# Row 0 of the first x transfer as a transfer of its own, ahead of rows 1 to 3, with y left whole

## Chip, cores, metric

One core of a Trainium2 chip. The metric is the device time of one execution in microseconds (us), the lower the better. All runs told of here were in the undisturbed ("fast") state. A difference of under 2% counts as "same".

## The reference

```python
x, y: float32 [1024, 4096]
out[r] = sum over c of abs(x[r, c] - y[r, c])      # float32 [1024]
```

Two inputs of 16.8 MB each go in, 4 KB come out. Almost nothing is computed per byte.

## The kernel before

Each of the 128 partitions holds 8 rows. The kernel has buffers on chip for all 8 rows of x (`xa` rows 0 to 3, `xb` rows 4 to 7), but only for 4 rows of y (`yb`). Rows 4 to 7 of y are loaded into the slots of rows 0 to 3 when those have been subtracted. VectorE subtracts in place, ScalarE takes the absolute value and sums.

```python
PIECES = [1728, 1056, 640, 384, 288]          # the last row comes in pieces
...
# first instructions of SyncE and ScalarE: 4 rows each, 64 KB a partition
put(lambda: nc.sync.dma_start(out=xa, in_=xr[:, 0:H, :]).then_inc(s_first, 16), before="RegisterMove")
put(lambda: nc.scalar.dma_start(out=yb, in_=yr[:, 0:H, :]).then_inc(s_first, 16), before="RegisterMove")
# next on SyncE: rows 4 to 6 of x, 48 KB a partition, no wait
put(lambda: nc.sync.dma_start(out=xb[:, 0:H - 1, :], in_=xr[:, H:K - 1, :]).then_inc(s_xb, 16))
for k in range(H - 1):                        # y rows 4 to 6, each when its slot is free
    put(lambda: nc.sync.wait_ge(s_sub, k + 1))
    put(lambda: nc.sync.dma_start(out=yb[:, k, :], in_=yr[:, H + k, :]).then_inc(s_row[k], 16))
...                                           # then row 7 of both in pieces
for k in range(H):
    sub(xa[:, k, :], yb[:, k, :], [(s_first, 32)] if k == 0 else [])
    absum(xa[:, k, :], ro[:, k:k + 1], s_act)
...                                           # rows 4 to 7 the same way, then 4 KB out
```

A transfer that has landed has raised its semaphore (a counter that engines wait for) by 16, so a wait for 32 on `s_first` is a wait for two whole transfers.

A transfer is cut over 16 DMA engines, 8 partitions each. What an engine moves for one partition in one transfer is one packet in the trace: 64 KB for `xa` and `yb`, 48 KB for the next x transfer.

Of the kernel before, what the change touches and what calls it, by code (L numbers as in the profile page):

```python
# [5 lines left out]

F32 = mybir.dt.float32
ABS = mybir.ActivationFunctionType.Abs
AX = mybir.AxisListType.X

F32 = mybir.dt.float32
ABS = mybir.ActivationFunctionType.Abs
AX = mybir.AxisListType.X

PIECES = [1728, 1056, 640, 384, 288]
HALVES = [2048, 2048]


class Entry:


    def __init__(self, nc):
        self.nc = nc

    def put(self, emit, before="UnconditionalBranch"):
        nc = self.nc
        hook = nc.inst_callbacks[-1]
        lower = nc._always_lower_symbolic_ap
        nc.remove_inst_callback(hook)
        nc._always_lower_symbolic_ap = False  # L30
        here = nc.cur_bb.bb.instructions
        n = len(here)
        try:
            emit()
        finally:
            nc._always_lower_symbolic_ap = lower
            nc.push_inst_callback(hook)
        here = nc.cur_bb.bb.instructions
        main = nc.main_func.blocks[0].instructions
        while len(here) > n:  # L40
            mine = here.pop(n)
            first = next(i for i, x in enumerate(main) if x.engine == mine.engine and x.opcode == before)
            main.insert(first, mine)

    def at_end(self, emit):

        nc = self.nc
        hook = nc.inst_callbacks[-1]
        here = nc.cur_bb.bb.name
        done = []  # L50

        def closing(ins):
            if done or nc.cur_bb.bb.name == here or ins.engine != mybir.EngineType.SP:
                return
            done.append(ins)
            emit()

        nc.remove_inst_callback(hook)
        nc.push_inst_callback(closing)
        nc.push_inst_callback(hook)  # L60


@with_exitstack
def kernel(ctx, tc, x, y, axis, out):
    nc = tc.nc
    P = nc.NUM_PARTITIONS
    R, C = x.shape
    K = R // P
    xr = x.rearrange("(p k) c -> p k c", p=P, k=K)
    yr = y.rearrange("(p k) c -> p k c", p=P, k=K)  # L70
    orr = out.rearrange("(p k) -> p k", p=P, k=K)
    assert sum(PIECES) == C and sum(HALVES) == C
    n_part = len(PIECES) - 1
    n2 = len(HALVES)
    H = K // 2
    entry = Entry(nc)
    put = entry.put

    def sbuf(name, shape):
        return nc.alloc_sbuf_tensor(name, shape, F32).ap()  # L80

    xa = sbuf("xa_rows", [P, H, C])
    xb = sbuf("xb_rows", [P, H, C])

    yb = sbuf("yb_rows", [P, H, C])
    ro = sbuf("ro_sums", [P, K])
    half = sbuf("half_sums", [P, 2, n2])

    last = sbuf("last_piece", [P, n_part + PIECES[-1]])

    s_first = tc.alloc_semaphore("s_first")
    s_xb = tc.alloc_semaphore("s_xb")
    s_row = [tc.alloc_semaphore(f"s_row{k}") for k in range(H - 1)]
    s_piece = [tc.alloc_semaphore(f"s_piece{i}") for i in range(len(PIECES))]
    s_sub = tc.alloc_semaphore("s_sub")
    s_act = tc.alloc_semaphore("s_act")
    s_end = tc.alloc_semaphore("s_end")
    s_out = tc.alloc_semaphore("s_out")


    put(lambda: nc.sync.dma_start(out=xa, in_=xr[:, 0:H, :]).then_inc(s_first, 16), before="RegisterMove")
    put(lambda: nc.scalar.dma_start(out=yb, in_=yr[:, 0:H, :]).then_inc(s_first, 16), before="RegisterMove")
    put(lambda: nc.sync.dma_start(out=xb[:, 0:H - 1, :], in_=xr[:, H:K - 1, :]).then_inc(s_xb, 16))
    for k in range(H - 1):
        put(lambda: nc.sync.wait_ge(s_sub, k + 1))
        put(lambda: nc.sync.dma_start(out=yb[:, k, :], in_=yr[:, H + k, :]).then_inc(s_row[k], 16))
    o = 0
    for i, w in enumerate(PIECES):
        c = slice(o, o + w)
        put(lambda: nc.sync.dma_start(out=xb[:, H - 1, c], in_=xr[:, K - 1, c]).then_inc(s_piece[i], 16))  # L110
        if i == 0:
            put(lambda: nc.sync.wait_ge(s_sub, H))
        put(lambda: nc.sync.dma_start(out=yb[:, H - 1, c], in_=yr[:, K - 1, c]).then_inc(s_piece[i], 16))
        o += w


    count = [0, 0]

    def sub(tx, ty, waits):
        for s, v in waits:  # L120
            put(lambda: nc.vector.wait_ge(s, v))
        put(lambda: nc.vector.tensor_sub(out=tx, in0=tx, in1=ty).then_inc(s_sub, 1))  # L122
        count[0] += 1

    def absum(tx, to, sem):
        put(lambda: nc.scalar.wait_ge(s_sub, count[0]))
        put(lambda: nc.scalar.activation(tx, tx, ABS, accum_out=to).then_inc(sem, 1))  # L127
        count[1] += sem is s_act

    for k in range(H):  # L130
        sub(xa[:, k, :], yb[:, k, :], [(s_first, 32)] if k == 0 else [])
        absum(xa[:, k, :], ro[:, k:k + 1], s_act)
    sub(xb[:, 0, :], yb[:, 0, :], [(s_xb, 16), (s_row[0], 16)])
    absum(xb[:, 0, :], ro[:, H:H + 1], s_act)

    for k in (1, 2):
        o = 0
        for i, w in enumerate(HALVES):
            c = slice(o, o + w)
            sub(xb[:, k, c], yb[:, k, c], [(s_row[k], 16)] if i == 0 else [])  # L140
            absum(xb[:, k, c], half[:, k - 1, i:i + 1], s_act)
            o += w
    done56 = count[1]
    o = 0
    for i, w in enumerate(PIECES):
        c = slice(o, o + w)
        tx, ty = xb[:, H - 1, c], yb[:, H - 1, c]
        if i == 2:
            put(lambda: nc.vector.wait_ge(s_act, done56))
            put(lambda: nc.vector.reduce_sum(out=ro[:, K - 3:K - 1], in_=half, axis=AX).then_inc(s_end, 1))  # L150
        if i < n_part:
            sub(tx, ty, [(s_piece[i], 32)])
            absum(tx, last[:, i:i + 1], s_end)
        else:
            put(lambda: nc.vector.wait_ge(s_piece[i], 32))
            put(lambda: nc.vector.tensor_sub(out=last[:, n_part:n_part + w], in0=tx, in1=ty).then_inc(s_end, 1))  # L156
            put(lambda: nc.vector.wait_ge(s_end, n_part + 2))
            put(lambda: nc.vector.reduce_sum(out=ro[:, K - 1:K], in_=last, axis=AX, apply_absolute_value=True).then_inc(s_end, 1))  # L158
        o += w

    put(lambda: nc.sync.wait_ge(s_end, n_part + 3))
    put(lambda: nc.sync.dma_start(out=orr, in_=ro).then_inc(s_out, 16))
    entry.at_end(lambda: nc.sync.wait_ge(s_out, 16))


# [1 line left out]
_INS = ['x', 'y', 'axis']  # L167
_OUTS = [((1024,), 'float32')]

_NUMBERS = {'axis': -1}  # L170


# [26 lines left out]
```

## Time and profile before

| | before |
|---|---|
| time, median of 3 | 85.63 us (85.59 to 85.64) |
| bytes read | 33.55 MB |
| rate over the span of 83.7 us | 401 GB/s |
| VectorE busy, ScalarE busy | 36.3 us, 31.6 us |
| first subtraction starts | 41.39 us |

The table says "limited by reading": each compute engine is idle for more than half of the span. How the single views carry that is told in the prediction. A stretch counts a packet's bytes at the packet's start, so a short stretch with long packets can show 519 or 371 GB/s for the same flow; only long stretches, or the packet records one by one, can be compared. The chain of waits names what released an instruction, not what it queued behind.

### The profile page before, as it was taken

Reading aid. Unit: us, or ns where it says so; the run is one execution under the profiler, and the core shown is the slowest. Engines: PE = TensorE matmul, PEld = TensorE weight load, DVE = VectorE, ACT = ScalarE, POOL = GpSimd, SP = SyncE. Lnnn points to the kernel's source line nnn. Section 1 sums busy time; section 2 is a strip of 40 time slices with the busy share of each in tenths; the row PEclk is TensorE's granted clock in tenths of the full one; section 3 lists DMA queues with packets and bytes.
Section 4 is the critical chain, followed back from the end, with each engine's and each line's share of the span. In section 5 each row is a group of like instructions: output and inputs, shape, how many; then the busy total and the mean of one; then the engine's idle time right before and its main releaser. Section 6 shows DMA issues by size and latency. Waiting matters only on the chain.

```text
span 83.7 us, 102 instructions
## 1 busy us (share of the span) xinstructions
DVE 36.3 (43%) x16; ACT 31.6 (38%) x27; POOL 0.2 (0%) x4
## 2 busy tenths in 40 slices
DVE  0000000000000000000299999999199898997870
ACT  5000000000000000000000979798880899999960
POOL 0000000000000000000000000000000000000000
DMA  9569999983999999669899988889999999999910
GB/s 501 219 282 501 501 501 501 501 376 157 470 501 501 501 501 438 282 282 501 376 399 634 470 376 376 376 360 438 438 399 462 407 454 377 423 409 410 392 40 2
DMA packets 2449, 33.56 MB, mean 401 GB/s; under 512 B 401, under 2 KB 913, under 8 KB 1681
## 3 DMA queue, kind: packets, MB, share of 16 engines
q1 hardware_dynamic: 2304, 25.17, 71.5%
q10 hardware_dynamic: 144, 8.39, 23.1%
q14 instruction: 1, 0.00, 0.0%
HBM read 33.55 MB, written 0.00 MB: 401 GB/s over the span
## 4 chain that ended last, share of the span: by engine, by line
DMA 68%; DVE 22%; ACT 7%; ACTq 0%; issue 0%
DMA yb_rows<-in_y_dram 68%; DVE xa_rows L122 16%; ACT xb_rows L127 7%; DVE xb_rows L122 5%; DVE ro_sums L158 1%; ACTq L194 0%
## 5 line engine op out<-in xcount | busy, mean ns | idle before, releaser
L122 DVE TENSOR_TENSOR xa_rows<-xa_rows,yb_rows 128x4096 f32<-128x4096 f32 x4 | 17.4, 4420 | 41.4 <-DMA yb_rows<-in_y_dram 41.4
L127 ACT ACTIVATE xa_rows<-xa_rows 128x4096 f32<-128x4096 f32 x4 | 14.5, 3616 | 45.5 <-DVE xa_rows L122 45.5
L122 DVE TENSOR_TENSOR xb_rows<-xb_rows,yb_rows 128x2048 f32<-128x2048 f32 (+5 forms) x9 | 17.9, 2020 | 3.4 <-DMA yb_rows<-in_y_dram 3.3
L127 ACT ACTIVATE xb_rows<-xb_rows 128x2048 f32<-128x2048 f32 (+5 forms) x9 | 15.2, 1686 | 2.9 <-DVE xb_rows L122 2.8
L127 ACT ACTIVATION_READ_ACCUMULATOR xb_rows<-xb_rows 128x1 f32 x9 | 1.7, 186 | 0.0
L127 ACT ACT_TABLE_LOAD x1 | 1.3, 1283 | 0.9 <-PEq L180 0.9
L127 ACT ACTIVATION_READ_ACCUMULATOR xa_rows<-xa_rows 128x1 f32 x4 | 0.7, 186 | 0.0
L156 DVE TENSOR_TENSOR last_piece<-xb_rows,yb_rows 128x288 f32<-128x288 f32 x1 | 0.5, 459 | 0.2 <-DMA yb_rows<-in_y_dram 0.2
L158 DVE TENSOR_REDUCE ro_sums<-last_piece 128x1 f32<-128x292 f32 x1 | 0.5, 457 | 0.1
L150 DVE TENSOR_REDUCE ro_sums<-half_sums 128x2 f32<-128x4 f32 x1 | 0.1, 150 | 0.0
L180 POOL MEMSET const-bfloat16-1.0<- 128x1 bf16 x1 | 0.1, 102 | 0.0
L180 POOL MEMSET const-uint8-127<- 128x1 uint8 x1 | 0.1, 102 | 0.0
L180 POOL MEMSET const-float32-1.0<- 128x1 f32 x1 | 0.1, 99 | 0.0
L180 POOL MEMSET const-float32-0.0<- 128x1 f32 x1 | 0.1, 98 | 0.2 <-issue 0.2
## 6 DMA issues: line engine op xcount, KB each, us to landing
xb_rows<-in_x_dram SPq DMA_DIRECT2D x1, 6144.0 KB, 54.8
yb_rows<-in_y_dram SPq DMA_DIRECT2D x3, 2048.0 KB, 15.3
xb_rows<-in_x_dram SPq DMA_DIRECT2D x1, 864.0 KB, 17.6
yb_rows<-in_y_dram SPq DMA_DIRECT2D x1, 864.0 KB, 15.8
xb_rows<-in_x_dram SPq DMA_DIRECT2D x1, 528.0 KB, 16.7
yb_rows<-in_y_dram SPq DMA_DIRECT2D x1, 528.0 KB, 17.5
xb_rows<-in_x_dram SPq DMA_DIRECT2D x1, 320.0 KB, 17.8
yb_rows<-in_y_dram SPq DMA_DIRECT2D x1, 320.0 KB, 18.1
```

The lines of the kernel that those rows point to most:

```text
L122: put(lambda: nc.vector.tensor_sub(out=tx, in0=tx, in1=ty).then_inc(s_sub, 1))
L127: put(lambda: nc.scalar.activation(tx, tx, ABS, accum_out=to).then_inc(sem, 1))
L150: put(lambda: nc.vector.reduce_sum(out=ro[:, K - 3:K - 1], in_=half, axis=AX).then_inc(s_end, 1))
L156: put(lambda: nc.vector.tensor_sub(out=last[:, n_part:n_part + w], in0=tx, in1=ty).then_inc(s_end, 1))
L158: put(lambda: nc.vector.reduce_sum(out=ro[:, K - 1:K], in_=last, axis=AX, apply_absolute_value=True).then_inc(s_end, 1))
L180: nc = _bacc.Bacc("TRN2", target_bir_lowering=False, num_devices=1)
```

## The change

The intent, as the code shows it: row 0 of x comes in short packets, so it is on chip early. The wait still asks for everything.

```diff
-    put(lambda: nc.sync.dma_start(out=xa, in_=xr[:, 0:H, :]).then_inc(s_first, 16), before="RegisterMove")
-    put(lambda: nc.scalar.dma_start(out=yb, in_=yr[:, 0:H, :]).then_inc(s_first, 16), before="RegisterMove")
+    for r in (slice(0, 1), slice(1, H)):
+        put(lambda: nc.sync.dma_start(out=xa[:, r, :], in_=xr[:, r, :]).then_inc(s_first, 16), before="Drain")
+    put(lambda: nc.scalar.dma_start(out=yb, in_=yr[:, 0:H, :]).then_inc(s_first, 16), before="Drain")
...
-        sub(xa[:, k, :], yb[:, k, :], [(s_first, 32)] if k == 0 else [])
+        sub(xa[:, k, :], yb[:, k, :], [(s_first, 48)] if k == 0 else [])
```

## The prediction

> **What bounds the kernel now.** I read the page first (busy shares, the forty slices, the DMA issues), then the chain of waits, then the transfers in stretches that I chose by where the chain breaks, and last the single packet records of the trace. The page clears the compute engines at once:
>
> ```profile
> DVE 36.3 (43%) x16; ACT 31.6 (38%) x27; POOL 0.2 (0%) x4
> ...
> DMA  9569999983999999669899988889999999999910
> ...
> HBM read 33.55 MB, written 0.00 MB: 401 GB/s over the span
> ```
>
> VectorE and ScalarE are idle more than half the time, and the DMA row is near 9 nearly everywhere. The 5, 6 and 3 in that row look like holes, but a slice is 2.09 us and a 64 KB packet takes longer than that; a whole packet is counted where it starts, so the row beats against the packet length. Stretches much longer than a packet take the beat out:
>
> ```profile
> core 0: us, DVE busy (x) ACT busy (x) POOL busy (x), PEclk, DMA share, GB/s
> 0.00:1.00 1.00, 0.00 (x0) 0.09 (x1) 0.20 (x4) 1.00 0.00 0
> 1.00:4.00 3.00, 0.00 (x0) 1.20 (x1) 0.00 (x0) 1.00 1.09 371
> 4.00:40.00 36.00, 0.00 (x0) 0.00 (x0) 0.00 (x0) 1.00 1.00 435
> 40.00:56.00 16.00, 14.61 (x4) 8.90 (x5) 0.00 (x0) 1.00 0.99 426
> 56.00:70.00 14.00, 11.72 (x4) 10.78 (x7) 0.00 (x0) 1.00 1.00 427
> 70.00:80.00 10.00, 8.84 (x8) 9.71 (x13) 0.00 (x0) 1.00 0.99 398
> ```
>
> From 1 us to 80 us the 16 DMA engines have a share of 0.99 to 1.00 (1.09 in the start is a packet counted past its stretch). There are no holes; only the rate falls, slowly, as packets get smaller towards the end. The chain of waits tells which landings matter:
>
> ```profile
> 0.13 41.24 DMA yb_rows<-in_y_dram
> 41.37 0.02 issue
> 41.39 13.11 DVE xa_rows L122 x3
> 54.49 0.02 issue
> 54.51 15.88 DMA yb_rows<-in_y_dram
> 70.39 0.02 issue
> 70.41 4.51 DVE xb_rows L122 x2
> ```
>
> It must be read with care. It says that three subtractions release a y transfer at 54.51 that lands 15.88 us later. But that transfer is 2 MB, which takes 4.9 us at 427 GB/s; the other 11 us it stands behind others in the same queue. So the subtractions are not what sets the time there; the queue is. The idle time of the first subtraction after the first rows says the same:
>
> ```profile
> L122 DVE TENSOR_TENSOR xb_rows<-xb_rows,yb_rows 128x4096 f32<-128x4096 f32 x1 | 4.4, 4424 | 1.9 <-DMA yb_rows<-in_y_dram 1.9
> ```
>
> VectorE works through the first four rows and then waits 1.9 us for the next. The first landing, taken as a signal, could slip by up to that with nothing lost. What can't slip is the stream of bytes: anything that makes it longer moves the end one for one.
>
> **What the Trainium skill says.** In "DMA: Bandwidth & Descriptors", section "Queues, rings and completion order", each DMA engine goes round between the queue rows that have work and switches only at packet boundaries. The records agree: on one engine a 64 KB packet of the SyncE queue (x) is followed by one of the ScalarE queue (y), in strict turn, each starting within 5 ns of the end of the one before. The same page, "Where 436 GB/s comes from", gives 435 GB/s for the 16 engines together; the trace has 435 in the stretch 4 to 40 us, so there is no speed left to win in steady state. Its section "Why small descriptors are slow" gives a fixed few cycles per packet; the trace shows how small that is here (below). In "Perfetto Trace Analysis", section "DMA Optimizations", splitting DMAs may help where DMA engines are idle and parts can start sooner; neither holds here, as the next part shows.
>
> **The change part by part.** Removed: one x transfer of 8 MB (128 packets of 64 KB, 8 an engine). Added: two x transfers in its place, row 0 (8 packets of 16 KB an engine) and rows 1 to 3 (8 of 48 KB an engine). Bytes, order inside the SyncE queue, and y are as before.
>
> Start position: the placement in the diff also goes from before the first RegisterMove to before the first Drain. In the built programs no RegisterMove is left and the transfers are the first instruction of SyncE and of ScalarE in both, followed by the Drain. I count 0.
>
> Compute: the instruction order of VectorE and ScalarE is unchanged. The first subtraction waits for 48 instead of 32, that is, for both x parts and y. So row 0, though it lands early, releases nothing. Gain there: 0.
>
> Issue: SyncE issues one more transfer, 0.38 us in the timeline, and reaches the barrier, and the next x transfer, that much later: at about 1.3 instead of 0.91 us. That transfer isn't served before 40 us. Cost on the path: 0.
>
> Turns: before, x and y packets alternate at equal size and finish together near 40.5 us. After, 8 turns of 16 KB against 64 KB: y is done after 8 x (607 + 2414) ns = 24.2 us of service, near 26 us, with row 0. Then the SyncE queue runs alone with rows 1 to 3 for 8 x 1812 ns = 14.5 us. A lone queue is not slower: between 40 and 56 us it is alone, with 48 KB packets at 1812 ns, that is 27.1 GB/s an engine, the same as the 64 KB packets in turn (65536 B in 2414 ns). These three paces, 2414, 1812 and 607 ns from start to start, are medians of the packet records.
>
> Sum for an engine: before 16 x 2414 = 38624 ns. After 8 x 607 + 8 x 2414 + 8 x 1812 = 4856 + 19312 + 14496 = 38664 ns, so 40 ns more, for 8 more packets. One more completion packet is 6 ns (its pace in the records). Together 0.05 us. The first subtraction should start near 41.45 instead of 41.39, and now be released by x. Every later landing moves by about the same, and so does the end: 85.63 + 0.05 = 85.68 us. I say 85.7.
>
> **The rivals.** First, the start. The first x packet of an engine takes 2.89 to 3.44 us in the records, where later ones of the same size take 2.42: some 0.65 us at the middle that steady state does not have, and the reason why the stretch 1 to 4 us moved only 371 GB/s. If that loss belongs to the first packet in proportion to its size, a 16 KB first packet loses a quarter, 0.16 us, and 0.49 us is won: 85.2 us. If it is a fixed ramp (all engines starting together, the first reads), it stays, only spread over the 16 KB packet and the y packet behind it. I hold the second likelier: no other first packet of a transfer shows an extra (the first 48 KB packet took 1815 ns like the rest), so it belongs to the moment, not to the packet. Second, unequal packets: turns by packet give y four times the bytes of x, and if an engine lost time fetching descriptors for short packets, 8 short ones an engine could cost some 0.1 us each at worst: 0.8 us, 86.5. Against it: the 16 KB packets after 55 us run alone at 607 ns with no gap. Third, an early start of compute: row 0 of x is on chip near 26 us, as is all of y, and a kernel that waited for row 0 alone could start 15 us earlier. This one doesn't, and even if it did, the queue would still set the end: the y slots would be free earlier, but the queue is never empty now. So this rival makes 85.7 as well, not less. Fourth, the placement: if something of a few tenths ran ahead of the transfers, all would move, to perhaps 86.0; the built programs speak against it.
>
> **Range and chances.** The three runs before spread over 0.05 us. The sum gives 85.7; a partly cured ramp pulls down by up to 0.5, a placement or descriptor cost pulls up by some tenths. I take 85.3 to 86.0 for 8 in 10. A 2% verdict needs 1.7 us, more than every rival above makes; within 2% gets 0.97, slower 0.02 and faster 0.01.
>
> **What would show it right or wrong.** Right: in the chain the first piece is now the x transfer, landing near 41.3 us after the issue; y lands near 26.5; the stretch 4 to 40 us still shows 435 GB/s; the wait of 1.9 us before the fifth row is still there; the last landing moves by under 0.1 us. Wrong: a faster 1 to 4 us (the ramp scales with the packet), a rate below 430 GB/s between 4 and 26 us (short packets cost) or between 26 and 40 us (x alone reads more slowly), or a first packet later than 1.0 us after the first issue (placement). A change of over 1.7 us either way would mean that the stream itself had a limit that this trace, with equal packets in two queues, did not show.

## The result, and the profile after

| | before | after |
|---|---|---|
| median of 6 runs each | 85.61 us (85.49 to 85.70) | 85.35 us (85.20 to 85.57) |
| ratio | | 0.9976, 95% interval 0.9958 to 0.9994 |
| first subtraction starts | 41.39 us | 41.09 us |

A ratio here is the mean time of one kernel's fast runs over that of the other's fast runs of the same rounds, so it isn't quite the ratio of the medians. By it the change is worth -0.2 us (85.6 x 0.0024), anywhere from -0.05 to -0.36: "same" by the 2% rule, but on the other side of zero than the predicted +0.05.

The transfers of the changed kernel in stretches, with the columns of the view before (stretch, its length, busy time of VectorE, ScalarE, GpSimd, clock, DMA share, GB/s):

```profile
1.00:4.00 3.00, 0.00 (x0) 1.28 (x1) 0.00 (x0) 1.00 1.38 519
4.00:40.00 36.00, 0.00 (x0) 0.00 (x0) 0.00 (x0) 1.00 0.98 422
40.00:56.00 16.00, 14.91 (x4) 9.20 (x5) 0.00 (x0) 1.00 0.99 426
56.00:70.00 14.00, 11.44 (x4) 10.60 (x7) 0.00 (x0) 1.00 1.00 429
70.00:80.00 10.00, 8.91 (x7) 9.71 (x13) 0.00 (x0) 1.00 0.99 396
```

519 and 422 are not a faster start and a slower middle: more packets start before 4 us now, so bytes are booked in the first row that were in the second before. Taken together, 1 to 40 us has (3 x 519 + 36 x 422) / 39 = 429 GB/s, and (3 x 371 + 36 x 435) / 39 = 430 GB/s before: the same flow. From 40 us on the rows differ by 2 GB/s at most. A finer cut of the same trace gives the part in which x is alone:

```profile
25.50:40.00 14.50, 0.00 (x0) 0.00 (x0) 0.00 (x0) 1.00 1.00 434
```

x alone in one queue runs as fast as both queues together. The chain of waits (start, length, what):

```profile
0.43 40.64 DMA xa_rows<-in_x_dram
41.06 0.02 issue
41.09 13.11 DVE xa_rows L123 x3
54.19 0.02 issue
54.21 16.06 DMA yb_rows<-in_y_dram
70.27 0.02 issue
70.30 4.51 DVE xb_rows L123 x2
```

The first piece is the second x transfer now, in place of y. The first subtraction starts 0.30 us earlier, and the subtraction at 70.30 only 0.11 us earlier (70.41 before). In between, y row 4 is waited for a bit longer than the 1.9 us of before:

```profile
L123 DVE TENSOR_TENSOR xb_rows<-xb_rows,yb_rows 128x4096 f32<-128x4096 f32 x1 | 4.4, 4426 | 2.1 <-DMA yb_rows<-in_y_dram 2.1
```

So most of the 0.30 us runs into that wait, as it must where the stream and not the landing counts. The list of transfers (issuer, KB, us from issue to landing) holds one surprise:

```profile
xa_rows<-in_x_dram SPq DMA_DIRECT2D x1, 6144.0 KB, 40.6
...
xa_rows<-in_x_dram SPq DMA_DIRECT2D x1, 2048.0 KB, 24.1
...
yb_rows<-in_y_dram ACTq DMA_DIRECT2D x1, 28.2
```

y lands 28.2 us after its issue at 0.12, at 28.3 us, though its last data packet ends at 26.11 us in the packet records. Its completion packets (4 bytes, 9 ns) start at 27.57 to 27.92 us: each had to wait for its turn behind a 48 KB packet of x, 1.8 us long. Here nobody waits for y alone, so it costs nothing.

**Where the 0.2 us comes from, as far as the packets show it.** The packet records allow a sum for an average engine: the time at which it reaches the next x transfer (rows 4 to 6), less the service of all packets ahead of it at their paces. What is left, called the start figure below, is the first start (1.12 us on average before, 1.15 after) plus what the start loses. Before: 40.51 - 38.64 = 1.87 us. After: 40.42 - 38.68 = 1.74 us. The start figure is 0.13 us smaller, and the packets cost the 0.05 us more that the prediction counted. The slowest of the 16 engines, which decides when a transfer has landed, reaches it at 40.61 instead of 40.80 us; in a second profile of each program order, told of below, it is 40.70 and 40.82. These are single profiles; how far they repeat is seen in the table of all lengths below. The first packets show where: 16 KB packets take 0.96 to 1.53 us on most engines where 0.61 is their pace, so they lose 0.5 us or so at the middle, against 0.65 for the 64 KB ones.

### The profile page after: what moved, and what is told of

It reads as the page before. It is cut to its first block, busy times and chain, and to the rows that moved or that the text cites. A ratio compares the mean times of both kernels' runs of the same rounds, so it can differ in the third digit from the quotient of the medians.

```text
span 83.6 us, 103 instructions
## 1 busy us (share of the span) xinstructions
DVE 36.3 (43%) x16; ACT 31.6 (38%) x27; POOL 0.2 (0%) x4
## 4 chain that ended last, share of the span: by engine, by line
DMA 68%; DVE 22%; ACT 7%; ACTq 0%; SPq 0%; issue 0%
DMA xa_rows<-in_x_dram 49%; DMA yb_rows<-in_y_dram 19%; DVE xa_rows L123 16%; ACT xb_rows L128 7%; DVE xb_rows L123 5%; DVE ro_sums L159 1%; ACTq L195 0%; SPq L102 0%
## 6 DMA issues: line engine op xcount, KB each, us to landing
xa_rows<-in_x_dram SPq DMA_DIRECT2D x1, 2048.0 KB, 24.1
```

## The experiments

Theory: the end is set by the stream of bytes, and the small gain is a cheaper start with short first packets. Rivals: the changed placement; the split itself or the queues ending apart; the early landing; and, for all, chance, since single runs differ by 0.2 us. The runs came in three sets on three chips; each set has its own runs of the kernel before.

### Placement alone

The kernel before with `before="RegisterMove"` replaced by `before="Drain"` in both first transfers; nothing else.

> The kernel before with only the placement word changed (first transfers ahead of the Drain instead of the RegisterMove). Each engine's instructions stand in the same order in the built programs. My theory (the gain of 0.26 us comes from the smaller first packets in the start-up): 85.6 us, ratio 1.000 within 0.0015, first packets again 2.9 to 3.4 us, so this run also shows how far two equal programs differ. Rival (placement): if it carries the gain, 85.35 us, ratio 0.997.

Measured: 85.60 us beside 85.57, ratio 1.0004 (0.9989 to 1.0019). The start figure is 1.89 us, that of the kernel before, and first packets take 2.47 to 3.35 us, 3.09 at the middle as before. Placement has no effect that this can see, as the equal orders of the built programs said. It also shows how wide two equal programs spread: 85.46 to 85.84 us in 16 runs.

### The changed kernel again

> The changed kernel once more, with more rounds, beside the placement run on one chip. If the small gain is real: ratio 0.996 to 0.999, first subtraction near 41.1 us. If it was chance between runs: ratio 0.999 to 1.001.

Measured: median 85.47 beside 85.57, ratio 0.9992 (0.9971 to 1.0013). The middle lies in the range for chance and the interval covers both ranges, so the time doesn't tell the two expectations apart; the gain in time is not confirmed by this run. The first subtraction came at 41.13 us, as expected, and the start figure is 1.67 us, again low. But one of the six runs took 85.93 us, and it is the profiled one. Its flow after the start is slower than the changed kernel's first profile, in the stretch 56 to 65 us. First the changed kernel's first profile, then this run:

```profile
56.00:65.00 9.00, 6.94 (x2) 5.64 (x4) 0.00 (x0) 1.00 1.02 437
```
```profile
56.00:65.00 9.00, 6.75 (x2) 5.67 (x4) 0.00 (x0) 1.00 1.00 419
```

The same instructions, the same packets, 4% fewer bytes for 9 us. Such runs come in other kernels too (85.84 us for the kernel before in this set) and are as large as the effect. That is why the packet records of the start are used as a witness beside the time.

### The long x packets first

```diff
-    for r in (slice(0, 1), slice(1, H)):
+    for r in (slice(0, H - 1), slice(H - 1, H)):
```

> The changed kernel with the two x transfers the other way round: rows 0 to 2 first (48 KB packets), then row 3 (16 KB packets). Same number of transfers, packets and issues. Theory (the size of the first packet decides how much the start-up loses): most of the gain is gone, first packets take about 2.3 us, 85.55 us, ratio 0.999 to 1.001. Rival (it is the split itself, or that y ends early and x alone is left): same as the changed kernel, 85.35 us, ratio 0.997.

Measured: 85.59 us, ratio 0.9997 (0.9983 to 1.0012), start figure 1.91 us, first packets 2.49 us at the middle. As many transfers, packets and issues as in the changed kernel, and y again ends ahead of x; the gain in the start is gone. So the split as such and the queues ending apart don't bring it. This rests on the start figure: by time, 0.9997 is not told from the 0.9992 of the changed kernel in this set.

### Both first transfers split

```diff
-    put(lambda: nc.scalar.dma_start(out=yb, in_=yr[:, 0:H, :]).then_inc(s_first, 16), before="Drain")
+    for r in (slice(0, 1), slice(1, H)):
+        put(lambda: nc.scalar.dma_start(out=yb[:, r, :], in_=yr[:, r, :]).then_inc(s_first, 16), before="Drain")
...
-[(s_first, 48)]
+[(s_first, 64)]
```

> Both first transfers as row 0 (16 KB) and rows 1 to 3 (48 KB). Theory: first packets 16 KB, so the start-up gain as in the changed kernel, with one more 0.05 us of packet cost, and x and y ending together again: 85.4 us, ratio 0.997 to 0.999. Rival (the gain comes from y ending early, its completion out of the way): gain gone, 85.65 us.

Measured: 85.42 us, ratio 0.9981 (0.9967 to 0.9994), start figure 1.73 us. As the theory has it. And an unplanned proof came along. Its chain of waits, and the row of the subtraction of row 4:

```profile
0.52 42.38 DMA yb_rows<-in_y_dram
42.90 0.02 issue
42.92 13.11 DVE xa_rows L124 x3
56.02 0.02 issue
56.04 14.27 DMA yb_rows<-in_y_dram
70.31 0.02 issue
70.33 4.50 DVE xb_rows L124 x2
```
```profile
L124 DVE TENSOR_TENSOR xb_rows<-xb_rows,yb_rows 128x4096 f32<-128x4096 f32 x1 | 4.4, 4426 | 0.3 <-DMA yb_rows<-in_y_dram 0.3
```

The completion of y stood behind a 48 KB packet again, and this time the first subtraction waits for it: it starts at 42.92 instead of 41.39 us. All y rows are asked for 1.5 us later. Yet the subtraction at 70.33 is as early as in the changed kernel; only the wait before row 4 shrank, from 1.9 to 0.3 us. The chain shows the y transfer as 14.27 us where it was 15.88: it shortened by what the issue was late. It had only been standing in the queue.

### A later first subtraction

On the kernel before: a clear of an unused buffer ahead of the first subtraction, behind the same wait.

```diff
+    junk = sbuf("junk", [P, 1280])
+    put(lambda: nc.vector.wait_ge(s_first, 32))
+    put(lambda: nc.vector.memset(junk, 0.0))
     for k in range(H):
```

> The kernel before with a clear of an unused buffer (128x1280) put ahead of the first subtraction on VectorE, behind the same wait: the first subtraction starts 0.7 to 1.4 us later. Theory (the stream of bytes sets the end and the first landing has 1.9 us of slack): 85.6 us, ratio 0.999 to 1.001, and the wait before the fifth row shrinks by what was added. Rival (the chain of waits as printed, in which the first subtractions release the y rows that end the kernel): 86.3 to 87.0 us.

```profile
41.72 1.12 DVE junk L132
42.84 17.29 DVE xa_rows L122 x4
```
```profile
L122 DVE TENSOR_TENSOR xb_rows<-xb_rows,yb_rows 128x4096 f32<-128x4096 f32 x1 | 4.4, 4425 | 0.6 <-DMA yb_rows<-in_y_dram 0.6
```

The subtractions start 1.4 us later (42.8 against 41.4), the wait before row 4 is 0.6 instead of 1.9 us, and the time is 85.68 us, ratio 1.0010 (0.9990 to 1.0030): at most 0.26 us of the 1.4 us, most likely none or 0.1. The rival (86.3 and more) is out. Slack at this place is shown, by this and by the split of both.

### Row 0 alone releases the first subtraction

Row 0 of x and y raise `s_first` (32 in all), rows 1 to 3 raise a semaphore of their own for which the second subtraction waits.

```diff
+    s_rest = tc.alloc_semaphore("s_rest")
...
-        put(lambda: nc.sync.dma_start(out=xa[:, r, :], in_=xr[:, r, :]).then_inc(s_first, 16), before="Drain")
+        put(lambda: nc.sync.dma_start(out=xa[:, r, :], in_=xr[:, r, :]).then_inc(s_rest if r.start else s_first, 16), before="Drain")
...
-[(s_first, 48)] if k == 0 else []
+[(s_first, 32)] if k == 0 else [(s_rest, 16)] if k == 1 else []
```

> The changed kernel, but the first subtraction waits for y and row 0 of x alone (32), the second for rows 1 to 3. Theory (stream-bound): the first subtraction starts near 28 us instead of 41, one y row is asked for 17 us earlier, and the end stays where the changed kernel has it: ratio to before 0.996 to 1.000. Rival (an early start shortens the work after the last bytes): 84 us or less.

The instructions of VectorE in order of time (start, length, [idle before]):

```profile
28.37 4.43 DVE L124 TENSOR_TENSOR xa_rows<-xa_rows,yb_rows 128x4096 f32<-128x4096 f32 x1 [28.37 <-DMA yb_rows<-in_y_dram]
41.08 13.10 DVE L124 TENSOR_TENSOR xa_rows<-xa_rows,yb_rows 128x4096 f32<-128x4096 f32 x3 [8.29 <-DMA xa_rows<-in_x_dram]
60.62 4.42 DVE L124 TENSOR_TENSOR xb_rows<-xb_rows,yb_rows 128x4096 f32<-128x4096 f32 x1 [6.44 <-DMA yb_rows<-in_y_dram]
```

The first subtraction starts 13 us earlier than before, and row 4 starts at 60.62 us against 60.70: the work done early turns into idle time, 6.44 us of it. The first y row is asked for at 32.82 instead of 45.84 us, 13 us earlier and not the 17 expected. Four of the six runs took 85.31 to 85.40 us; two late ones (85.94 and 86.32) make the ratio 1.0012 (0.9977 to 1.0046), just past the expected edge. An early start gains nothing that is seen; it doesn't come near the rival's 84.

### The length of the first packets

Five cuts of x at another column, the changed kernel otherwise. x is taken as one row of 16384 elements a partition and cut at FIRST: 1024, 2048, 3072, 6144 or 8192.

```diff
-    for r in (slice(0, 1), slice(1, H)):
-        put(lambda: nc.sync.dma_start(out=xa[:, r, :], in_=xr[:, r, :]).then_inc(s_first, 16), before="Drain")
+    xf = xa.rearrange("p k c -> p (k c)")
+    xd = x.rearrange("(p k) c -> p (k c)", p=P, k=K)
+    for c in (slice(0, FIRST), slice(FIRST, H * C)):
+        put(lambda: nc.sync.dma_start(out=xf[:, c], in_=xd[:, c]).then_inc(s_first, 16), before="Drain")
```

4 KB:

> The changed kernel with the first cut of x at 1024 columns: 4 KB packets first, then 60 KB. Theory (what counts is how short the packets in the first 3 us are): the 60 KB packet comes right behind the 4 KB one, before y, so the start-up is as costly as with a long first packet: 85.6 us, ratio 0.999 to 1.001. Rival (the length of the very first packet alone counts): at least the gain of the changed kernel, 85.35 us, ratio 0.996 to 0.998.

32 KB:

> The changed kernel with x cut in halves: 32 KB packets, then 32 KB. Theory (start-up loss falls with the length of the first packets): between the two, 85.5 us, ratio 0.998 to 1.000, stream of an average engine reaches the next x transfer some 0.05 us earlier than in the kernel before. Rival (a threshold below 48 KB): the full gain of 0.15 us or none.

8 KB:

> First cut of x at 2048 columns: 8 KB packets, then 56 KB. 4 KB and 32 KB gave nothing and 16 KB gave 0.1 to 0.2 us. Theory (a best length around 16 KB): between, 85.45 to 85.55 us, ratio 0.998 to 1.001. Rival (16 KB is special and its neighbours are not): 85.6 us, start loss as before.

24 KB:

> First cut of x at 6144 columns: 24 KB packets, then 40 KB. Theory (a best length around 16 KB): half the gain of 16 KB, 85.5 us, ratio 0.998 to 1.000. Rival (16 KB special): none, 85.6 us.

12 KB:

> First cut of x at 3072 columns: 12 KB packets, then 52 KB. Theory (a best length around 16 KB): nearly the gain of 16 KB, 85.4 us, ratio 0.997 to 0.999. Rival (16 KB special): none, 85.6 us.

All kernels by the length of their first x packets, with the start figure worked out as above from one profile each (for lengths that no long run of packets shows, the pace is interpolated between 607 ns for 16 KB and 2414 ns for 64 KB):

| first x packets | start figure, average engine (us) | time and ratio to the kernel before |
|---|---|---|
| 4 KB | 1.84 | 85.50, 1.0008 (0.9990 to 1.0026) |
| 8 KB | 1.84 | 85.43, 1.0006 (0.9993 to 1.0018) |
| 12 KB | 1.72 | 85.44, 1.0002 (0.9989 to 1.0016) |
| 16 KB (changed kernel, twice; both split; row 0 alone) | 1.74, 1.67; 1.73; 1.72 | ratios 0.9976, 0.9992; 0.9981; 1.0012 |
| 24 KB | 1.67 | 85.32, 0.9993 (0.9981 to 1.0006) |
| 32 KB | 1.86 | 85.46, 1.0001 (0.9983 to 1.0018) |
| 48 KB | 1.91 | 85.59, 0.9997 (0.9983 to 1.0012) |
| 64 KB (before; placement; later subtraction; y split, told next) | 1.87; 1.89; 2.00; 1.85 | 1; 1.0004; 1.0010; 1.1411 |

The start figures fall in two groups without overlap: 1.67 to 1.74 us for 12 to 24 KB, 1.84 to 2.00 us for both shorter and longer ones. The expectation for 4 KB was right in its number and wrong in its reason: the 60 KB packet doesn't follow at once, because an engine has eight 4 KB packets, and six of them run before the first y packet. 32 KB was expected to have a part of the gain and has none: an average engine reaches the next x transfer at 40.54 us (40.51 before). 8 KB came out in the expected range of times, but its start is that of the kernel before, as its rival had it. Of the cuts beside 16 KB, 24 KB is as good in the start and better than expected; 12 KB has the good start but missed the expected 0.997 to 0.999. In its profile, the slowest of its five runs, one engine reached the next x transfer 0.56 us later than the average; whether that is the reason isn't shown. In the time, none of these five is told from the kernel before; 0.15 us is 0.0018, about the half width of an interval. Taken as groups, the ratios average 0.9993 for 12 to 24 KB (0.9996 without the first result, which began the search) and 1.0004 for the other lengths (y split left out): 0.1 us apart and on the side of the start figures. That is as far as the times carry it.

What makes 12 to 24 KB cheaper in the first two us is not shown by any of these runs. One thing in the packet records goes with it: in the six profiles of that group every engine serves exactly two x packets before its first y packet. With 32 KB and more it serves one, with 8 KB about four and with 4 KB mostly six. No run separates this count from the length, so it is a trace to follow and not a cause.

### y split, x whole

```diff
-    for r in (slice(0, 1), slice(1, H)):
-        put(lambda: nc.sync.dma_start(out=xa[:, r, :], in_=xr[:, r, :]).then_inc(s_first, 16), before="Drain")
-    put(lambda: nc.scalar.dma_start(out=yb, in_=yr[:, 0:H, :]).then_inc(s_first, 16), before="Drain")
+    put(lambda: nc.sync.dma_start(out=xa, in_=xr[:, 0:H, :]).then_inc(s_first, 16), before="Drain")
+    for r in (slice(0, 1), slice(1, H)):
+        put(lambda: nc.scalar.dma_start(out=yb[:, r, :], in_=yr[:, r, :]).then_inc(s_first, 16), before="Drain")
```

> x stays one transfer of 64 KB packets, y goes as row 0 (16 KB) and rows 1 to 3 (48 KB). Theory (the gain of about 0.18 us sits in the first x packets of 16 KB, served before any y): no gain, an average engine loses some 0.7 us in the start as before, 85.6 us, ratio 0.999 to 1.001. Rival (short y packets, or the queues ending apart, bring it): 85.4 us, ratio 0.997 to 0.999.

Measured: 97.42 us beside 85.36, ratio 1.1411 (1.1395 to 1.1426). Both expectations missed by 12 us. What they were about can still be read: the start figure is 1.85 us, as with the other 64 KB first packets, so short y packets behind them bring nothing. The mirror image of a harmless change is the worst kernel. Its transfers (KB, us to landing) and two stretches:

```profile
yb_rows<-in_y_dram ACTq DMA_DIRECT2D x1, 6144.0 KB, 55.4
xb_rows<-in_x_dram SPq DMA_DIRECT2D x1, 6144.0 KB, 54.4
...
yb_rows<-in_y_dram ACTq DMA_DIRECT2D x1, 2048.0 KB, 26.7
...
xa_rows<-in_x_dram SPq DMA_DIRECT2D x1, 26.5
```
```profile
26.00:55.00 29.00, 0.00 (x0) 0.00 (x0) 0.00 (x0) 1.00 0.96 417
55.00:61.00 6.00, 5.05 (x2) 0.59 (x1) 0.00 (x0) 1.00 0.00 0
```

Turns go by packet, so for eight turns x gets 64 KB against 16 KB of y. x is complete at 26.5 us, with one row of y. Behind x in its queue stands the next x transfer, which waits for nobody, and it goes turn about with rows 1 to 3 of y at equal size, 48 KB. So y is complete only when rows 4 to 6 of x are too: 1.9 + 8 x (2.414 + 0.607) + 8 x (1.812 + 1.812) = 55.1 us by the paces. The first subtraction starts at 55.95 us. Until then no y slot is free and nothing more can be asked for, so the queues run dry: 0 GB/s from 55 to 61 us. From there on VectorE is the bound:

```profile
L123 DVE TENSOR_TENSOR xa_rows<-xa_rows,yb_rows 128x4096 f32<-128x4096 f32 x4 | 17.4, 4420 | 56.0 <-DMA yb_rows<-in_y_dram 56.0
...
L123 DVE TENSOR_TENSOR xb_rows<-xb_rows,yb_rows 128x4096 f32<-128x4096 f32 x1 | 4.4, 4418 | 0.0
```

The wait before row 4 is 0.0 now. 55.95 us and VectorE's 35.7 us of work make 91.7, and the span is 95.7; the rest is 1.8 us in which VectorE waits for the last sums of ScalarE, and the output. The first subtraction is 14.6 us late (55.95 less 41.39), the time 12.1 us: the slack at the first landing is used up, and the rest is paid.

## Why the prediction was right, and where it was off

- **The bound** (a stream of bytes, 1.9 us of slack at the first landing, the chain of waits to be read with care): right, and shown three times: a start of the subtractions 1.4 to 1.5 us later costs nothing that is seen, one of 13 us earlier gains nothing, one of 14.6 us later costs 12.1.
- **Placement 0, compute 0, issue 0**: right. Placement alone gave 1.0004; the next x transfer is issued at 1.26 us (1.3 predicted) and served after 40 us.
- **x alone is not slower**: right, 434 GB/s from 25.5 us on. The prediction's own border, 26 us, gives 411 GB/s, under its sign of being wrong (430); but it gives 403 before, and x's 48 KB packets keep their 1812 ns there, so this is the booking of packets at their start.
- **Packet cost +0.05 us**: not measurable by itself in the time, but the sum of paces with it leaves start figures that agree among kernels with 16 KB first packets within 0.07 us.
- **The first rival, dismissed too far.** The step that failed is "If it is a fixed ramp [...] it stays": the change of the start loss was taken as 0 and is -0.13 to -0.2 us with 16 KB packets (start figure 1.67 to 1.74 against 1.87 and 1.89). The proportional version (-0.49) was wrong as well: 4 and 8 KB save nothing. With it the sum is +0.05 - 0.13 = -0.08 us for an average engine of the profiled run; the slowest engine is 0.19 us earlier in all, near the measured -0.2, in one profile of each. So the first subtraction came at 41.09 us and not at 41.45, and the last landing is 0.13 us earlier (80.30 against 80.43) where "under 0.1 us" was said. The range 85.3 to 86.0 held 85.35 only because it allowed for a part of this, and by 0.05 us: two of the six runs lie below it. That it held is in part luck; the sum had the sign wrong.
- **y lands near 26.5**: wrong, 28.3 us. The data end was right (26.11 us); the completion packet's turn behind a 48 KB packet was not thought of. Row 0 of x was to be done with y near 26 us; it landed at 24.1, since two of its packets ran before the first of y.
- **"The stretch 4 to 40 us still shows 435"**: it shows 422, and means nothing: the check was put on a border at which packets of another length are booked elsewhere. For the same reason the 371 GB/s of 1 to 4 us, which the prediction took for the start loss, can't be read as one; the length of the first packets can.
- **A rival not seen at all**: the prediction wrote that y gets four times the bytes of x, and asked only whether short packets cost. It didn't ask who is served first, and why that is harmless here: y, served first, has nothing behind it in its queue, so the rest of x, which is waited for, runs alone. y split alone shows the other case, +12 us.

## What to carry to other kernels

Where two queues share the DMA engines, the packet length is the share: give the longer packets to the queue whose data is waited for and which has nothing useful to follow, and not to the one that can run ahead into later data; here the wrong way round cost 12.1 us. In a kernel bound by its stream, test slack by making the first consumer late before believing a chain of waits; and if a kernel waits for one queue alone, allow for one packet of the other queue between the last byte and its completion (1.8 us for a 48 KB packet, in two kernels here). An effect of 0.2 us among runs that spread by 0.2 us is easier to see in the packet records of several profiles than in the times, and what it is worth in time stays uncertain.

## What the Trainium skill lacked or had wrong

- "DMA: Bandwidth & Descriptors", "Queues, rings and completion order": says that turns go by packet, not what follows from it. Unequal packets split the bytes unequally, and it can cost 12.1 us of 85.4 (y split, x whole: 97.42 us).
- The same section: gives a packet as some 9 to 17 descriptors, and no page has its bytes for transfers issued from SyncE or ScalarE on this chip; what the records here show as one packet is all that one transfer moves for one partition, up to 65536 bytes in 2414 ns, which makes the turn long.
- The same page, "Anatomy of one DMA" (told for transfers issued from GpSimd): the completion's delay is put on the write receipt. Here, with transfers issued from SyncE and ScalarE, the completion packet itself waits for a turn behind the other queue's packet: last data at 26.11 us, completion packets from 27.57 us, landing at 28.3 us.
- The same page, "Latency and other measured facts": gives about 600 ns to the first byte for transfers issued from SyncE or ScalarE, but not from where it counts; here the first packets start 1.0 us after the start of the issue and 0.62 us after its end at 0.38.
- No page has the loss at the start of a stream: first packets of 64 KB take 2.89 to 3.44 us in the kernel before, against 2.42 later, and the loss is 0.1 to 0.2 us smaller with first packets of 12 to 24 KB than with shorter or longer ones. Its cause is open.
- The same page, "Specifications": about 27 GiB/s an engine; the records have 65536 bytes in 2414 ns, 27.1 GB/s, which fits the page's 435 GB/s for 16 engines and not the GiB.
